# A two-layer attention backbone: transposes between the layers into the score banks, and a second `hf` buffer

## The chip, the cores and the metric

The kernel runs on one core of one Trainium2 chip. The metric is the device time of one execution, in microseconds (us); of several runs the median is told. Engines are named as in the profile: PE is TensorE (PEld its weight loads), DVE is VectorE, ACT is ScalarE, POOL is GpSimd, SP is SyncE, which issues most DMAs.

## The reference, cut to what matters

A residual stream of 512 latent tokens and 256 context tokens, each 1024 wide, passes two layers. Layer 0 is differential attention, layer 1 grouped-query attention. Each layer normalises the stream, scales and shifts it by values derived from a conditioning vector, mixes it, and adds a normalised, gated result back:

```python
for i in range(DEPTH):
    h = rms_norm(x, pre_g[i]) * (1.0 + scale) + shift
    hc = rms_norm(xc, pre_g[i]) * (1.0 + cscale) + cshift
    ...                                     # y, yc = attention(h, hc) @ w_out
    x = x + gate * rms_norm(y, post_g[i])
    if not last:
        xc = xc + cgate * rms_norm(yc, post_g[i])
```

Everything is float32. The change lies where layer 0's last two lines meet layer 1's first two.

## The kernel before, in words

Tokens are worked on in six tiles of 128 (0 to 3 latent, 4 and 5 context). A float32 product is made of three matmuls on operands split in a high and a low part (`mm3`, L142 to L145: high by high, high by low, low by high), so every weight and every activation is cast to its high part on ACT and has its low part made by a subtraction on DVE or POOL (L203 and L204 for weights).

**PSUM.** The eight banks are divided by hand (L120, L121): four single banks `bk`, and two score tiles `sc` of two banks each. The four single banks are handed out in turn from a list `lru`: `pj` (L129) takes the bank at its head for an accumulation and `close` (L135) puts it back at the end after its readers were issued; `trp` (L124) takes the head for transposes and puts it at the end at once. `sc2` (L138) hands out the two score tiles in turn. Score tiles serve the attention scores, the opening's transposes (L568) and the first four output projections of layer 0 (L1069).

**The stage of the change.** After layer 0's attention, `w_out` is applied in three column groups (256, 256 and 512 wide). The last group's loop (L1254 to L1263) goes over the six token tiles. For tile i it takes a bank, multiplies the first four of eight row blocks (12 matmuls), transposes the first half of tile i-2 (`h1_tr(.., 0)`), multiplies the other four blocks, calls `resid_a` (L1210: sum of squares on ACT, multiplication by the gate into `u` on DVE, then the bank is closed), transposes the second half of tile i-2, and calls `resid_b` (L1222: the new residual on DVE, its sum of squares on ACT, the reciprocal root and the normalised tokens `xn` on POOL).

`h1_tr(m, j)` (L1237) turns half j of the normalised tile m (four blocks of 128 columns) to feature-major form: four transposes on PE into one bank (L1241), then scale and shift per block into the SBUF buffer `hf`, two blocks on DVE (L1247, HFD = 2) and two on ACT (L1249), then the cast of all four to the high part on ACT (L1251) and the subtraction for the low part on DVE (L1252). `hf` exists once (`bufs=1`).

Tiles 4 and 5 are transposed later, inside the list `KV` (L44, loop from L1331), which orders layer 1's k projections ('k'), v projections ('v'), transposes of rotated keys ('c') and of tiles 4 and 5 ('t') by hand. Each k or v projection takes a bank with `pj` and needs `h1hi` and `h1lo` of its token tile, and the split weights 8 and 9 (k) or 10 and 11 (v), which come through weight slots that the last group of `w_out` leaves.

**What sets the order.** The program text gives each instruction a priority (its place in the text, moved ahead inside `hot` and `tc.high_priority`), and the framework's scheduler, which plans the whole program ahead by a timeline of its own, fixes each engine's order. On the chip every engine takes its instructions in that fixed order and waits on semaphores that the framework places.

Of the kernel before, what the change touches and what calls it, by code (L numbers as in the profile page):

```python
# [9 lines left out]
F32 = mybir.dt.float32  # L10
# [6 lines left out]
P = 128  # L17
# [59 lines left out]
def f32(ap):  # L77
    return ap.bitcast(F32)
# [3 lines left out]
def tile_backbone(  # L82
# [23 lines left out]
    def nm(s):  # L106
        uid[0] += 1
        return f"{s}_{uid[0]}"
# [15 lines left out]
    def trp():  # L124
        i = lru.pop(0)
        lru.append(i)
        return banks[i]
# [10 lines left out]
    def sc2():  # L138
        scs.append(scs.pop(0))
        return scs[-1]  # L140
# [1009 lines left out]
    bp = bp_stack.enter_context(tc.tile_pool(name="bp", bufs=1))  # L1150
# [71 lines left out]
    def resid_b(m):  # L1222
# [11 lines left out]
        nc.gpsimd.tensor_scalar(t, xd, r, 1.0, ALU.mult, ALU.mult)  # L1234
        xn[m] = t

    def h1_tr(m, j):  # L1237
        v = 0 if m < NQ else 1
        tr = trp()
        for k in range(4):  # L1240
            nc.tensor.transpose(tr[:, k * P:(k + 1) * P], xn[m][:, (j * 4 + k) * P:(j * 4 + k + 1) * P], ident)  # L1241
        hf = bp.tile([P, 4, P], F32, tag="hf", name=nm("hf"), bufs=1)
        for k in range(4):
            kt = j * 4 + k
            src, s_, h_ = tr[:, k * P:(k + 1) * P], mods[:, 1, v, 1, kt:kt + 1], mods[:, 1, v, 0, kt:kt + 1]
            if k < HFD:
                nc.vector.tensor_scalar(hf[:, k, :], src, s_, h_, ALU.mult, ALU.add)  # L1247
            else:
                nc.scalar.activation(hf[:, k, :], src, AF.Identity, scale=s_, bias=h_)  # L1249
        hs = h1hi[:, j * 4:j * 4 + 4, m * P:(m + 1) * P]  # L1250
        nc.scalar.copy(hs, hf)  # L1251
        nc.vector.tensor_tensor(h1lo[:, j * 4:j * 4 + 4, m * P:(m + 1) * P], hf, f32(hs), ALU.subtract)  # L1252

    for i, m in enumerate(order):  # L1254
        o = pj(n)
        run(out_proj(o, ghi, glo, w, m, n, 0, 4))
        if i >= 2:
            h1_tr(order[i - 2], 0)
        run(out_proj(o, ghi, glo, w, m, n, 4, 8))
        resid_a(m, o)  # L1260
        if i >= 2:
            h1_tr(order[i - 2], 1)
        resid_b(m)  # L1263
# [3 lines left out]
    with tc.tile_pool(name="t1", bufs=1, side="right") as t1p:  # L1267
# [63 lines left out]
        for what, m in KV:  # L1331
            if what == "t":
                hot(h1_tr, m, 0)
                hot(h1_tr, m, 1)
            elif what == "c":
                k_tr(*ktr.pop(0))
            elif what == "g":
                gate1_acc()
            else:
                if what == "v" and wv is None:  # L1340
                    wv = (ws.get(10), ws.get(11))
                o = pj(256)
                run(proj_tok(o, wk if what == "k" else wv, m))
                if late:
                    k_rope(*late.pop())
                if what == "k":
                    late.append((m, o, head_rstd(o)))
                else:
                    nc.scalar.copy(vh[:, m, :], o)
                    nc.vector.tensor_tensor(vl[:, m, :], o, f32(vh[:, m, :]), ALU.subtract)  # L1350
                    close(o)
# [172 lines left out]
        for h in range(KT):  # L1524
            p, j = h // 2, h % 2
# [142 lines left out]
```

## Time and profile before

| | |
|---|---|
| median of three runs | 836.27 us (836.08 to 836.4) |
| the profiled execution | 835.36 us |
| its span in the trace | 833.4 us |
| mean granted TensorE clock | 0.992 |
| PE, DVE, ACT, POOL busy | 96%, 58%, 55%, 53% of the span |

The profile lists busy time per engine, groups of equal instructions, waits (who waited for whom, and which instruction ended the wait) and instructions in order of time. An output is named before its inputs, `bk<-ident,xn` being a transpose of `xn` into a single bank; buffer numbers are left out. In windows, a row gives a stretch of time and each engine's busy time in it. A wait for several semaphores is put down to the one that came last. Ends of matmuls are modelled, so that those that run one behind the other overlap on paper.

### The profile page before, as it was taken

How to read it: one execution, taken by the hardware profiler on the slowest of the kernel's cores; microseconds unless marked ns; L12 is line 12 of the kernel's file. 1: busy time of each engine (PE TensorE's matmuls, PEld its weight loads, DVE VectorE, ACT ScalarE, POOL GpSimd, SP SyncE). 2: the span in 40 equal slices, each digit the busy share in tenths (PEclk: the TensorE clock that was granted, in tenths of full speed). 3: DMA queues.
4: the chain of work that ended last, by engine and by line, in shares of the span. 5: the costliest groups of instructions: out<-in, count | busy, mean ns of one | idle time of the engine just before them, and what ended most of it. 6: DMA issues, size and time to landing. Idle time of an engine off the chain costs nothing. (4 is left out here: it accounts for less than half of the span.)

```text
span 833.4 us, 14405 instructions
## 1 busy us (share of the span) xinstructions
PE 797.3 (96%) x5482; PEld 705.0 (85%) x5482; DVE 482.7 (58%) x897; ACT 457.5 (55%) x1001; POOL 438.2 (53%) x538
## 2 busy tenths in 40 slices
PE   7999999999999999999999999789999999999997
PEld 5688887798878898778988898678999889899986
DVE  4434576764857525674477857566346656665634
ACT  5424357674574644764467642575355665666731
POOL 4444755865475843765733202576677755543201
PEclk9899999999999999999999999999999999999999
DMA  9934211122233321414310066040221210210212
GB/s 300 351 116 140 76 39 42 63 99 66 75 102 125 116 76 64 143 48 154 126 51 26 27 242 212 1 133 25 78 77 52 77 51 1 77 51 26 66 36 101
DMA packets 41540, 77.77 MB, mean 93 GB/s; under 512 B 3584, under 2 KB 18688, under 8 KB 41472
## 3 DMA queue, kind: packets, MB, share of 16 engines
q1 hardware_dynamic: 38048, 71.71, 25.8%
q10 hardware_dynamic: 3424, 5.15, 1.8%
q8 instruction: 43, 0.70, 0.4%
q14 instruction: 25, 0.20, 0.1%
HBM read 70.56 MB, written 2.10 MB: 87 GB/s over the span
## 5 line engine op out<-in xcount | busy, mean ns | idle before, releaser
L197 POOL TENSOR_TENSOR wlo<-raw,whi 128x256 fp32r<-128x256 f32 x200 | 148.9, 776 | 89.5 <-ACT whi L203 81.0
L143 PE MATMUL bk<-whi,h 128*128 128x256 f32 (+1 forms) x592 | 177.3, 302 | 7.7 <-ACT hf L1249 4.9
L144 PE MATMUL bk<-wlo,h 128*128 128x256 f32 (+1 forms) x592 | 177.0, 300 | 0.2 <-DVE wlo L197 0.2
L145 PE MATMUL bk<-whi,h 128*128 128x256 f32 (+1 forms) x592 | 175.8, 300 | 1.0 <-DVE h L1252 1.0
L143 PE MATMUL bk<-h,whi 128*128 128x512 f32 (+2 forms) x416 | 147.5, 355 | 2.1 <-ACT sq L962 1.5
L144 PE MATMUL bk<-h,whi 128*128 128x512 f32 (+2 forms) x416 | 144.9, 349 | 0.0
L145 PE MATMUL bk<-h,wlo 128*128 128x512 f32 (+2 forms) x416 | 144.8, 348 | 0.1
L143 PEld LDWEIGHTS bk<-whi,h 128*128 128x128 f32 x592 | 113.0, 191 | 18.0 <-ACT hf L1249 5.8
L144 PEld LDWEIGHTS bk<-wlo,h 128*128 128x128 f32 x592 | 113.0, 191 | 4.4 <-issue 0.5
L145 PEld LDWEIGHTS bk<-whi,h 128*128 128x128 f32 x592 | 112.1, 190 | 5.3 <-DVE h L1252 1.6
L211 POOL TENSOR_SCALAR p<-p,sm 128x768 f32<-128x768 f32 (+1 forms) x80 | 68.0, 852 | 81.8 <-DVE sm L876 34.5
L143 PEld LDWEIGHTS bk<-h,whi 128*128 128x128 f32 x416 | 78.2, 188 | 14.6 <-issue 4.5
L203 ACT CAST whi<-raw 128x1024 fp32r<-128x1024 f32 x64 | 67.2, 1050 | 36.9 <-PE bk L144 14.9
L145 PEld LDWEIGHTS bk<-h,wlo 128*128 128x128 f32 x416 | 78.1, 188 | 8.7 <-issue 1.3
L144 PEld LDWEIGHTS bk<-h,whi 128*128 128x128 f32 x416 | 78.3, 188 | 7.0 <-issue 0.8
L873 ACT ACTIVATE p<-sc,sm 128x768 f32<-128x768 f32 (+1 forms) x68 | 59.6, 880 | 29.4 <-DVE sm L870 28.6
L870 DVE TENSOR_REDUCE sm<-sc 128x1 f32<-128x768 f32 (+1 forms) x68 | 60.5, 919 | 22.0 <-PE sc L865 22.0
L1457 DVE TENSOR_TENSOR al<-bk,ah 128x512 fp32r<-128x512 f32 x48 | 32.3, 687 | 33.4 <-ACT ah L1456 33.2
L933 ACT CAST ah<-bk 128x512 fp32r<-128x512 f32 x56 | 31.7, 591 | 29.7 <-PE bk L930 23.3
L934 DVE TENSOR_TENSOR al<-bk,ah 128x512 fp32r<-128x512 f32 x56 | 37.6, 684 | 16.4 <-ACT ah L933 15.9
L865 PE MATMUL sc<-qk,qk 64*128 64x384 f32 (+1 forms) x396 | 46.1, 355 | 0.2 <-POOL qk L765 0.2
L181 POOL TENSOR_TENSOR sz<-sz,za 128x384 f32<-128x384 f32 (+1 forms) x24 | 28.1, 1174 | 32.9 <-ACT za L180 32.9
(245 smaller groups left out, 1697.4 us busy)
## 6 DMA issues: line engine op xcount, KB each, us to landing
raw<-in_a_w SPq DMA_DIRECT2D x30, 512.0 KB, 3.5
araw<-in_ada_w SPq DMA_DIRECT2D x12, 1024.0 KB, 5.3
raw<-in_b_w SPq DMA_DIRECT2D x20, 512.0 KB, 3.5
ag<-in_ada_w SPq DMA_DIRECT2D x32, 256.0 KB, 6.9
raw<-in_w_out SPq DMA_DIRECT2D x16, 512.0 KB, 3.5
sw<-qr ACTq DMA_DIRECT2D x32, 128.0 KB, 2.1
gw<-in_ada_w SPq DMA_DIRECT2D x8, 512.0 KB, 4.3
xt<-in_x SPq DMA_DIRECT2D x4, 512.0 KB, 5.4
```

The costliest lines, as they stand in the source:

```text
L143: nc.tensor.matmul(o, ahi, bhi, start=start, stop=False)
L144: nc.tensor.matmul(o, ahi, blo, start=False, stop=False)
L145: nc.tensor.matmul(o, alo, bhi, start=False, stop=stop)
L197: eng.tensor_tensor(dst[:, i:i + n], a[:, i:i + n], b[:, i:i + n], op)
L203: nc.scalar.copy(hi, r)
L211: (nc.vector if eng == "v" else nc.gpsimd).tensor_scalar(dst, src, s_, 1.0, ALU.mult, ALU.mult)
L865: prev = nc.tensor.matmul(sc[m][:, j if nk == T else m, :w], a[r, tok], b[r, c], start=i == 0, stop=i == 2)
L870: nc.vector.tensor_reduce(mx, scv, AX.XY if nk == T else AX.X, ALU.max, negate=True)
L873: nc.scalar.activation(pv_, scv, AF.Exp, bias=mx, accum_out=l[:, m:m + 1])
L933: nc.scalar.copy(ah, tr)
L934: nc.vector.tensor_tensor(al, tr, f32(ah), ALU.subtract)
L1457: nc.vector.tensor_tensor(al, tr, f32(ah), ALU.subtract)
```

## The change

`h1_tr` no longer takes a bank from the four with `trp`. With the first half of a tile it takes a score tile with `sc2`; the first half's transposes go to the first bank of that tile and the second half's to the second. The SBUF buffer `hf` exists twice. Nothing else in the text differs.

```diff
+    h1_ps = {}
+
     def h1_tr(m, j):
         v = 0 if m < NQ else 1
-        tr = trp()
+        if j == 0:
+            h1_ps[m] = sc2()
+        tr = h1_ps[m][:, j, :]
         for k in range(4):
             nc.tensor.transpose(tr[:, k * P:(k + 1) * P], xn[m][:, (j * 4 + k) * P:(j * 4 + k + 1) * P], ident)
-        hf = bp.tile([P, 4, P], F32, tag="hf", name=nm("hf"), bufs=1)
+        hf = bp.tile([P, 4, P], F32, tag="hf", name=nm("hf"), bufs=2)
```

## The prediction, made before the result was known

> **What bounds the kernel now.** I read the page first, then the stage between the layers by windows, then what TensorE waits for there, then its order of time.
>
> ```profile
> span 833.4 us, 14405 instructions
> ...
> PE 797.3 (96%) x5482; PEld 705.0 (85%) x5482; DVE 482.7 (58%) x897; ACT 457.5 (55%) x1001; POOL 438.2 (53%) x538
> ```
>
> ```profile
> 490.00:525.00 35.00, 34.69 (x207) 30.40 (x206) 22.11 (x35) 10.63 (x36) 9.98 (x21) 1.00 0.69 240
> 525.00:580.00 55.00, 46.49 (x305) 40.55 (x304) 36.01 (x78) 34.47 (x93) 36.39 (x56) 0.97 0.16 52
> 580.00:600.00 20.00, 20.00 (x170) 20.00 (x169) 4.74 (x15) 7.07 (x21) 12.07 (x21) 1.00 0.32 103
> ```
>
> The page first: TensorE (PE) is busy 96% of an 833.4 us span, so the whole kernel is a queue of matmuls and only its gaps are for sale. The windows (columns: stretch, length, then busy time and instructions of PE, PEld, DVE, ACT, POOL, then granted clock) show where one lies. Before 525 us PE is busy 34.69 of 35 us and from 580 us all 20 of 20. Between them it is busy 46.49 of 55: 8.5 us of gaps, in the stretch that the change touches. No other engine is full there: DVE 36.01 of 55 (65%), ACT 34.47 (63%). The stage is a chain of waits, not of work. Whose waits:
>
> ```profile
> PE bk L143 <- ACT hf L1249: 4.9, 4, 3.8
> PE bk L143 <- DVE u L1214: 1.1, 1, 1.1
> PE bk L145 <- DVE h L1252: 1.0, 3, 0.4
> PE bk L1241 <- DVE u L1214: 0.7, 1, 0.7
> PE bk L143 <- ACT h L1251: 0.6, 1, 0.6
> PE bk L1311 <- DVE kn L1321: 0.2, 1, 0.2
> ```
>
> Columns are microseconds in total, times, longest. A matmul of L143 opens an accumulation in a fresh bank and reads no `hf`; so "L143 <- ACT hf" can only mean that its bank still held transposed tokens that ACT had not read. The same goes for "<- DVE u" (a bank that still held a projection). These three rows, 4.9 + 1.1 + 0.7 = 6.7 us, are waits for a bank. The other three, 1.0 + 0.6 + 0.2 = 1.8 us, are waits for data: `h` itself, or a rotated key. The longest wait alone is 3.8 us. Its story in order of time (start, duration):
>
> ```profile
> 525.31 1.04 PE L1241 MATMUL bk<-ident,xn 128*128 128x128 f32 x8
> 526.62 0.72 DVE L1247 TENSOR_SCALAR hf<-bk,mods 128x128 f32<-128x128 f32 x2
> 527.43 0.80 ACT L1249 ACTIVATE hf<-bk,mods 128x128 f32<-128x128 f32 x2 [1.46 <-DVE hf L1247]
> 527.70 1.25 PE L1241 MATMUL bk<-ident,xn 128*128 128x128 f32 x8
> 529.66 0.60 ACT L1251 CAST h<-hf 128x512 fp32r<-128x512 f32 x1
> 530.30 0.69 DVE L1252 TENSOR_TENSOR h<-hf,h 128x512 fp32r<-128x512 f32 x1 [0.68 <-ACT h L1251]
> 531.10 0.73 DVE L1247 TENSOR_SCALAR hf<-bk,mods 128x128 f32<-128x128 f32 x2
> 531.92 0.81 ACT L1249 ACTIVATE hf<-bk,mods 128x128 f32<-128x128 f32 x2 [0.46 <-DVE hf L1247]
> 532.78 0.50 PE L143 MATMUL bk<-whi,h 128*128 128x512 f32 x1 [3.83 <-ACT hf L1249]
> 533.12 0.40 PE L144 MATMUL bk<-wlo,h 128*128 128x512 f32 x1
> 533.35 0.40 PE L145 MATMUL bk<-whi,h 128*128 128x512 f32 x1
> ```
>
> At 525.31 both halves of token tile 0 are transposed (eight transposes), each half in a bank of its own. DVE and ACT turn the first half into `hf` (526.62, 527.43), ACT casts it (529.66), DVE subtracts (530.30 to 530.99). Only then may the second half begin, since there is one `hf` buffer: DVE at 531.10, ACT from 531.92 to 532.73. PE had nothing since about 529, and starts token tile 4 at 532.78, 0.05 us after that read. Follow the four banks in the order in which they are handed out, calling them a to d: tile 0 takes a, tile 1 b, tile 2 c, its two transposes (of tile 0) d and a, tile 3 b, its transposes d and c, tile 4 again a. So tile 4 waits for the second half of tile 0 to leave bank a, and that half waits for the one `hf` buffer. The change takes away both links.
>
> **The change part by part.** *The banks.* The transposes keep their number and length; only their destination moves, and with it one claimant fewer turns the four banks: tile 4 then gets the bank of tile 0, finished long before. Are the score banks free?
>
> ```profile
> 493.00:600.00 107.00, 0.00 (x0) 0.00 (x0) 0.00 (x0) 0.00 (x0) 0.98 0.34 113
> ```
>
> That is the busy time of instructions that touch a score bank: none on any engine from 493 to 600 us. So all 6.7 us of bank waits lose their cause, since the first k projections also open in banks that only projections used.
>
> *The clock.* After the 3.8 us gap the granted clock fell:
>
> ```profile
> 534.00:537.20 3.20, 3.20 (x9) 2.43 (x9) 2.43 (x5) 1.93 (x6) 1.52 (x4) 0.50 0.00 0
> 550.00:580.00 30.00, 27.11 (x214) 25.38 (x214) 20.30 (x50) 17.82 (x52) 21.78 (x31) 1.00 0.19 59
> ```
>
> Half speed for 3.2 us is 1.6 us of matmul time. The stage's other waits are at most 1.1 us long by the rows of waits, and from 550 to 580 us, among several of them, the clock read 1.00. So when the long gap goes, this goes: 6.7 + 1.6 = 8.3 us.
>
> *The second `hf` buffer.* It adds no instruction. What it shortens is the conversion, whose work is in these groups of the stage (busy, mean ns of one, idle before); the last row, of the tile `hf`, has the first and last start:
>
> ```profile
> L1249 ACT ACTIVATE hf<-bk,mods 128x128 f32<-128x128 f32 x24 | 9.6, 453 | 10.1 <-DVE hf L1247 9.9
> L1252 DVE TENSOR_TENSOR h<-hf,h 128x512 fp32r<-128x512 f32 x12 | 9.1, 758 | 7.9 <-ACT h L1251 7.9
> L1247 DVE TENSOR_SCALAR hf<-bk,mods 128x128 f32<-128x128 f32 x24 | 8.7, 405 | 1.2 <-PE bk L1241 0.5
> L1251 ACT CAST h<-hf 128x512 fp32r<-128x512 f32 x12 | 7.4, 618 | 0.2
> L1247 DVE TENSOR_SCALAR hf<-bk,mods x24: 401/403/411, 526.6 to 575.0; 128x128 f32<-128x128 f32 x24
> ```
>
> Twelve halves cost DVE 8.7 + 9.1 = 17.8 us and ACT 9.6 + 7.4 = 17.0 us, so 1.5 us of each per half; through one buffer they came 4.4 us apart (526.6 to 575.0 in eleven steps). With two buffers the next half's first pass may run while the cast is on ACT.
>
> *What is late next.* PE now reaches the k projections about 8 us sooner, and these need `h`. The data waits of 1.8 us stay in the sum; how much they grow no row shows. From below it is nothing: in a stage of 55 - 8 = 47 us DVE would be busy 36.01/47 = 77% and ACT 73%, still short of full. From above it is all 8.3 us: if the conversion kept its old pace, the last of tile 3 would come when it did,
>
> ```profile
> 562.87 0.39 PE L145 MATMUL bk<-whi,h 128*128 128x256 f32 x1 [0.44 <-DVE h L1252]
> ```
>
> and PE would stand at the same k projection until 562.87 again. I take 2 us, near the low end, because both links of the old pace are cut and the shares stay under four fifths.
>
> *Waits that the change adds.* Both halves of a tile now share one two-bank score tile, and tiles m and m+2 share it in turn. Is a two-bank tile waited for by banks, or as one? The kernel's opening transposes into the same tiles:
>
> ```profile
> 10.28 0.68 DVE L578 COPY xnt<-sc 128x512 f32<-128x512 f32 x1
> 10.99 0.59 ACT L576 COPY xnt<-sc 128x512 f32<-128x512 f32 x1 [0.46 <-DVE xnt L578]
> 13.44 1.06 PE L571 MATMUL sc<-ident,xt 128*128 128x128 f32 x8 [0.34 <-DVE xt L211]
> 14.62 0.69 DVE L578 COPY xnt<-sc 128x512 f32<-128x512 f32 x1 [0.72 <-PE sc L571]
> ```
>
> DVE copies the first bank, ACT the second. At 10.99 ACT starts 0.03 us after DVE's copy ended, having idled 0.46 us for it, although it reads the other bank. At 14.62 DVE, idle 0.72 us, starts only after the last of all eight transposes (13.44 + 1.06 = 14.50), not after the four that fill its bank. So waits run by pair. Then the second half's transposes stand in PE's queue until the first half has been read (tile 0: from 525.8, half of the eight, to ACT's 527.43 + 0.80, 2.4 us). Behind them in that queue stand the matmuls of a later projection tile, and for these wait ACT's sum of squares, DVE's `u` and the next `xn`. Between a tile's two halves the program issues 12 matmuls of the projection; by the starts at 533.12 and 533.35 that is 12 x 0.23 = 2.8 us, which covers 2.4 us where the order of the program is kept. I count what is left of this inside the 2 us. [...]
>
> *Queues.* No DMA is added or moved in the text of the program; SP's loads of b_w and of the last context tile hang on weight slots and on `xn`, which PE frees sooner, so they come sooner with it.
>
> Sum: 8.3 - 2 = 6.3 us off the profiled execution. Its own time is 835.36 us (span 833.4 and 1.96 around it), which gives 829.1. The median of the runs before is 836.27, 0.9 above the profiled one; set off from that, the forecast is 830.0 us.
>
> **The rivals.** *All of it (by banks):* the pair costs nothing and the conversion keeps up: 836.3 - 8.3 = 828.0. For it: the engine shares. Against: the opening rows. Chance 0.13.
>
> *The weights are late:*
>
> ```profile
> 545.11 2.11 POOL L1234 TENSOR_SCALAR gate<-gate,sm 128x1024 f32<-128x1024 f32 x1
> 547.19 3.31 POOL L197 TENSOR_TENSOR wlo<-raw,whi 128x256 fp32r<-128x256 f32 x4
> 549.49 0.39 PE L143 MATMUL bk<-whi,h 128*128 128x256 f32 x1 [1.07 <-DVE u L1214]
> 556.36 3.27 POOL L197 TENSOR_TENSOR wlo<-raw,whi 128x256 fp32r<-128x256 f32 x4
> ```
>
> POOL's split of the second k weight runs until 550.50, a microsecond past the start of the k projections at 549.49, and the second v weight until 559.63. Both follow the last projection tile through a freed slot, so they move with it, but POOL makes the normalised tile 4 just ahead, and that took 2.11 us. One such wait at k and one at v, 1 to 2 us each, leave 2.3 to 4.3 us of the 6.3: about 833. Chance 0.17.
>
> *Nothing comes of it:* the conversion keeps its old pace because DVE and ACT take their instructions in an order in which the second buffer is not used; then only waits after 562.87 are saved: 836 us. Chance 0.09.
>
> *Slower:* the pair wait decides. If the second half's transposes are queued right behind the first half's (as at 525.31, eight in a row), each of six tiles holds PE for the 2.4 us above: 14.4 us against 8.3 gained, +6 us, 842. It turns from gain to loss where the wait passes 8.3 / 6 = 1.4 us per tile. Against it: the 12 matmuls between the halves in program order. Since the order of every later instruction is planned anew, a shift of layer 1 adds to this case. Chance 0.11.
>
> **How the numbers follow.** The forecast (829 to 832 us) has 0.50, with 0.13, 0.17, 0.09 and 0.11 for the rivals in their order. 0.2% is 1.7 us, about what a measurement of this kernel can tell from no change. Faster: 0.50 + 0.13 + 0.17 = 0.80; same 0.09; slower 0.11. The range runs from just below "all of it", 827.2, to the "nothing" case, 836.4; outside are the slower case and a tail below.
>
> **What would show it.** Right: in the profile after, no "L143 <- ACT hf" or "<- DVE u" among PE's waits of this stage, no window at half clock near 535, the first 256-wide matmul of the k projections at about 541 instead of 549.49, and the stage's PE gaps at 2 to 4 us. The pair wait would show as "PE L1241 <- ACT hf" with score tiles as outputs; the late weights as "L144 <- POOL wlo"; an unchanged conversion as starts of L1247 still 4.4 us apart. Wrong would be the forecast if the gaps went and the end did not move by the same amount, that is, if layer 1 gave it back.

## The result, and the profile after

The changed kernel took 829.37 us (median of 6 runs, 827.1 to 830.14) against 836.17 us for the kernel before (6 runs, 834.73 to 836.97). The ratio is 0.9916, with a 95% interval from 0.9904 to 0.9928: 6.8 us faster, where 6.3 had been forecast. The profiled execution took 828.93 us.

From line 1241 on, the lines of the changed kernel stand four further down: the transposes are L1245, `hf` is written at L1251 (DVE) and L1253 (ACT), `h` at L1255 and L1256.

First the page of the changed kernel: span and busy time.

```profile
span 827.1 us, 14389 instructions
PE 796.6 (96%) x5482; PEld 706.2 (85%) x5482; DVE 484.0 (59%) x897; ACT 455.5 (55%) x1001; POOL 437.2 (53%) x538
```

The span is 6.3 us shorter. PE was idle for 833.4 - 797.3 = 36.1 us before and for 827.1 - 796.6 = 30.5 us after: 5.6 us of the gain are idle time, 0.7 us busy time. Next the windows, in the columns of those before (stretch, length, PE, PEld, DVE, ACT, POOL, granted clock):

```profile
525.00:580.00 55.00, 51.89 (x353) 47.30 (x352) 38.53 (x80) 36.07 (x100) 40.19 (x61) 0.97 0.18 60
```

The gaps of PE between 525 and 580 us fell from 8.5 to 55 - 51.89 = 3.1 us, so 5.4 of the 5.6 us come from the stage that was changed. Who is still waited for there (total, times, longest):

```profile
PE bk L145 <- DVE h L1256: 2.0, 1, 2.0
PE bk L144 <- DVE wlo L197: 0.6, 1, 0.6
PE sc L1245 <- POOL gate L1234: 0.4, 1, 0.4
```

All three waits for a bank are gone (4.9 + 1.1 + 0.7 us before). The waits for data are 2.0 + 0.6 + 0.4 = 3.0 us, where they were 1.8. PE's order of time in the changed kernel, with the transposes of tiles 0 to 2, the first k projection and the row that ends the 2.0 us wait:

```profile
526.85 0.60 PE L1245 MATMUL sc<-ident,xn 128*128 128x128 f32 x4
...
531.71 0.60 PE L1245 MATMUL sc<-ident,xn 128*128 128x128 f32 x4
...
533.07 0.60 PE L1245 MATMUL sc<-ident,xn 128*128 128x128 f32 x4
...
540.04 0.60 PE L1245 MATMUL sc<-ident,xn 128*128 128x128 f32 x4
...
540.95 0.60 PE L1245 MATMUL sc<-ident,xn 128*128 128x128 f32 x4
...
541.62 0.40 PE L143 MATMUL bk<-whi,h 128*128 128x256 f32 x2
...
546.80 0.60 PE L1245 MATMUL sc<-ident,xn 128*128 128x128 f32 x4
...
555.56 0.39 PE L145 MATMUL bk<-whi,h 128*128 128x256 f32 x1 [2.03 <-DVE h L1256]
```

The k projections start at 541.62 us; before it was 549.49. But the halves of a tile, which stood together before (eight transposes at 525.31), are now far apart: tile 0 at 526.85 and 533.07, tile 1 at 531.71 and 540.95, tile 2 at 540.04 and 546.80. That has a consequence on SP's queue. The load of tile 5's context in the changed kernel, and then the same in the kernel before:

```profile
547.43 0.33 SPq L1219 DMA_DIRECT2D xn<-in_xc  x1
```

```profile
541.46 0.34 SPq L1219 DMA_DIRECT2D xn<-in_xc  x1
```

The load is written into the `xn` buffer that tile 2 leaves. Tile 2's last transpose ended at 546.80 + 0.60 = 547.40, and the load was issued 0.03 us later, 6 us later than before. VectorE's order in the changed kernel shows what that meets:

```profile
549.18 1.36 DVE L1251 TENSOR_SCALAR hf<-sc,mods 128x128 f32<-128x128 f32 x4
551.94 2.44 DVE L1228 SCALAR_TENSOR_TENSOR xn<-u,sm,xn 128x512 f32<-128x512 f32 x2 [1.41 <-DMA xn<-in_xc]
554.30 1.81 DVE L1256 TENSOR_TENSOR h<-hf,h 128x512 fp32r<-128x512 f32 x2
```

At 551.94 VectorE had idled 1.41 us for that load, with two subtractions for `h` queued behind it. The residual of tile 5 (L1228) took 2.44 us, the first subtraction began at 554.30, and PE waited for it until 555.56. Before, at the same instruction of VectorE:

```profile
551.33 1.42 DVE L1228 SCALAR_TENSOR_TENSOR xn<-u,sm,xn 128x512 f32<-128x512 f32 x2 [1.89 <-POOL sm L387]
```

There the two took 1.42 us, and no wait of PE for `h` in the stage was over 0.6 us.

### The profile page after: what moved, and what is told of

Its sections match the earlier page's. It is cut to its first block, busy times and chain, and to the rows that moved or that the text cites. A ratio compares the mean times of both kernels' runs of the same rounds, so it can differ in the third digit from the quotient of the medians.

```text
span 827.1 us, 14389 instructions
## 1 busy us (share of the span) xinstructions
PE 796.6 (96%) x5482; PEld 706.2 (85%) x5482; DVE 484.0 (59%) x897; ACT 455.5 (55%) x1001; POOL 437.2 (53%) x538
## 5 line engine op out<-in xcount | busy, mean ns | idle before, releaser
L197 POOL TENSOR_TENSOR wlo<-raw,whi 128x256 fp32r<-128x256 f32 x200 | 149.3, 779 | 81.1 <-ACT whi L203 71.8
L143 PEld LDWEIGHTS bk<-whi,h 128*128 128x128 f32 x592 | 112.7, 190 | 10.2 <-issue 4.2
```

Of the source, the lines that this page charges most:

```text
L143: nc.tensor.matmul(o, ahi, bhi, start=start, stop=False)
L197: eng.tensor_tensor(dst[:, i:i + n], a[:, i:i + n], b[:, i:i + n], op)
```

## The experiments

**Theories.** A, that of the prediction: the gain is the waits for single banks, and the second `hf` buffer only helps. B: the gain is the second buffer. Beside them stood the question of whether a score tile is waited for as a pair, and what that costs. Twelve runs were made: the table has ten of them, beside the two kernels compared, and two more (split_ktr with another `HFD`) stand further down. Each was made beside the kernel before on the same chip, which gave 835.9 to 836.4 us; ratios are to that, with 95% intervals.

| run | token transposes | key transposes | `hf` | us (median) | ratio |
|---|---|---|---|---|---|
| before | single banks | single banks | 1 | 836.2 | 1 |
| banks_only | pair in a score tile | single banks | 1 | 840.50 | 1.0026 to 1.0069 |
| buffer_only | single banks | single banks | 2 | 832.17 | 0.9938 to 0.9970 |
| after | pair in a score tile | single banks | 2 | 829.37 | 0.9904 to 0.9928 |
| split_tiles | two score tiles | single banks | 2 | 832.34 | 0.9938 to 0.9975 |
| forced_pair | pair, halves adjacent | single banks | 2 | 843.94 | 1.0072 to 1.0116 |
| forced_split | two score tiles, adjacent | single banks | 2 | 831.61 | 0.9929 to 0.9966 |
| x5_behind | as after | single banks | 2 | 830.71 | 0.9917 to 0.9963 |
| buffer_ktr | single banks | score tiles | 2 | 830.52 | 0.9914 to 0.9959 |
| ktr_score | pair in a score tile | score tiles | 2 | 828.05 | 0.9885 to 0.9915 |
| split_ktr | two score tiles | score tiles | 2 | 826.31 | 0.9864 to 0.9897 |
| after_again | as after | single banks | 2 | 827.72 | 0.9877 to 0.9922 |

### Each part alone: banks_only and buffer_only

banks_only takes the second buffer back, buffer_only the banks:

```diff
-        hf = bp.tile([P, 4, P], F32, tag="hf", name=nm("hf"), bufs=2)
+        hf = bp.tile([P, 4, P], F32, tag="hf", name=nm("hf"), bufs=1)
```

```diff
-        if j == 0:
-            h1_ps[m] = sc2()
-        tr = h1_ps[m][:, j, :]
+        tr = trp()
```

> The changed kernel with its transposes in the score tiles, but one hf buffer as before. Theory A (the gain is the bank waits of TensorE and the clock that fell after the longest): 829 to 831 us, the first k projection at 541 to 543 us, no L143 <- ACT hf among the waits; data waits on h grow by 1 to 2 us. Theory B (the gain is the second hf buffer): 835 to 837 us, since nothing that B counts is changed.

> The kernel before with the second hf buffer, its transposes still in the four single banks. Theory A in its strict form (a bank must be free, whoever frees it): the second half of tile 0 is read some 3 us earlier through the second buffer, so the 3.8 us wait shrinks to about 1 us, too short for the clock to fall; the waits for u stay: 831 to 833 us. Theory B (the buffer is all of the gain): 829 to 830 us. If the buffer is of no use alone: 836 us.

Neither theory held. The banks alone made the kernel 4.5 us slower (840.50 against 836.03 beside it), the buffer alone 3.9 us faster, and both together 6.8 us faster: the parts do not add up. Waits of PE in banks_only (500 to 600 us):

```profile
PE sc L1245 <- ACT hf L1253: 3.4, 1, 3.4
PE sc L1245 <- POOL xn L1234: 2.5, 1, 2.5
PE bk L144 <- DVE wlo L197: 2.2, 1, 2.2
```

The waits for single banks are gone here too, but L1245 waits 3.4 us for ACT to read the first half of a tile (at 561.74), and 2.5 us for `xn`. That is the wait for the pair, and the one buffer lets the first half be read only late. Most of the 4.5 us is clock, though. The stage's window:

```profile
525.00:580.00 55.00, 45.34 (x277) 40.21 (x276) 35.29 (x72) 30.72 (x85) 31.83 (x51) 0.91 0.15 51
```

PE's gaps are 55 - 45.34 = 9.7 us, only 1.2 more than the 8.5 before. But the granted clock is 0.91 where it was 0.97: 10.2 us at half clock in place of 3.4, which is up to 3.4 us more. The conversion itself got slower; VectorE's first pass over the halves in banks_only, in the changed kernel and in buffer_only (first and last start):

```profile
L1251 DVE TENSOR_SCALAR hf<-sc,mods x24: 396/402/411, 527.1 to 584.0; 128x128 f32<-128x128 f32 x24
```

```profile
L1251 DVE TENSOR_SCALAR hf<-sc,mods x24: 395/400/409, 528.0 to 568.6; 128x128 f32<-128x128 f32 x24
```

```profile
L1249 DVE TENSOR_SCALAR hf<-bk,mods x24: 394/402/411, 525.8 to 571.8; 128x128 f32<-128x128 f32 x24
```

Over eleven steps that is (584.0 - 527.1)/11 = 5.2 us from half to half in banks_only, 3.7 us after, 4.2 us in buffer_only, 4.4 us before. In buffer_only the 3.8 us wait has gone, and other waits for single banks have come:

```profile
PE bk L1243 <- POOL qrs L1302: 2.6, 1, 2.6
PE bk L1243 <- DVE kn L1323: 1.3, 1, 1.3
PE bk L143 <- ACT h L1253: 1.0, 1, 1.0
```

Two k projections hold their banks until POOL's `qrs` and VectorE's `kn` are done, and the transposes of tile 4 wait 2.6 and 1.3 us for them. So the buffer cures the wait of tile 4's projection, and the banks cure what then comes next; the banks need the buffer first.

### The wait for the pair: forced_pair and forced_split

In both, the halves of tiles 0 to 3 are transposed together, and the next projection's matmuls are ordered behind the second half. For that `h1_tr` returns its last transpose, which becomes `e1`. forced_pair keeps the score tile of the changed kernel; forced_split puts half j into score tile j. The loop of both, then what forced_split has besides:

```diff
     for i, m in enumerate(order):
         o = pj(n)
-        run(out_proj(o, ghi, glo, w, m, n, 0, 4))
+        with after(e1):
+            run(out_proj(o, ghi, glo, w, m, n, 0, 4))
         if i >= 2:
             h1_tr(order[i - 2], 0)
-        run(out_proj(o, ghi, glo, w, m, n, 4, 8))
+            e1 = h1_tr(order[i - 2], 1)
+        with after(e1):
+            run(out_proj(o, ghi, glo, w, m, n, 4, 8))
         resid_a(m, o)
-        if i >= 2:
-            h1_tr(order[i - 2], 1)
         resid_b(m)
```

```diff
-        if j == 0:
-            h1_ps[m] = sc2()
-        tr = h1_ps[m][:, j, :]
+        tr = scs[j][:, m % 2, :]
```

> The changed kernel with both halves of tiles 0 to 3 transposed together and TensorE's next projection matmuls ordered behind the second half. If a score tile is waited for as one (the slower rival of the prediction): TensorE stands 2.0 to 2.5 us at each second half, shown as L1245 <- ACT hf, four times, 8 to 10 us, and the clock falls after some: 836 to 842 us. If single banks are waited for: no such wait, 829 to 831 us.

> The kernel of forced_pair (halves of tiles 0 to 3 adjacent, the next projection matmuls behind them), but the halves in two different score tiles. If the 6.3 us of L1245 <- ACT hf in forced_pair (2.9, 1.7, 1.7) were the wait for the pair: that row is gone, and with two losses of clock the time falls by 6 to 10 us against forced_pair's 843.9, to 834 to 838 us; the 4.4 us wait for xn at 523.5 us, which the forced order causes, stays. If they came from the forced order: the waits stay, 842 to 844 us.

Waits of PE in forced_pair, then in forced_split:

```profile
PE sc L1245 <- ACT hf L1253: 6.3, 3, 2.9
PE sc L1245 <- POOL xn L1234: 5.4, 2, 4.4
```

```profile
PE sc L1243 <- POOL xn L1234: 4.4, 1, 4.4
```

With the pair, PE waits three times for ACT's reading of the first half, 2.9, 1.7 and 1.7 us (tile 3 kept 34 matmuls between its halves in the planned order). With two tiles that row is gone, and the time is 12.3 us lower, 2 us better than expected; half of that is the row itself, the rest half clock (10.2 us in this stage with the pair, 6.8 without) and waits further on. So a score tile is waited for as one, and a second half that has nothing ahead of it pays 1.7 to 2.9 us; the prediction had put it at 2.4.

### Halves in different tiles: split_tiles and split_ktr

split_tiles is the changed kernel with the second diff above alone. split_ktr also moves the transposes of rotated keys; ktr_score does only that:

```diff
-            tr = trp()
+            tr = sc2()[:, 0, :]
             for j in range(2):
                 nc.tensor.transpose(tr[:, j * P:(j + 1) * P], kr[:, j * P:(j + 1) * P], ident)
```

> The changed kernel, but the two halves of a token tile go to two different score tiles (half j to tile j, bank m % 2), so that a second half need not wait for the reading of the first. If the wait by pair costs time in the changed kernel (it sends second halves late: 6.2 us after the first for tile 0, 9.2 for tile 1; these delay tile 3's h and, through xn, the load of tile 5's context): the 2.0 us wait for h near 555 us and the half clock behind it (3.8 us, so 1.7 us lost) go, 826 to 828 us. If it costs nothing: 829.4 us as the changed kernel, within 0.8.

> split_tiles with the transposes of rotated keys in the score tiles too. split_tiles lost 1.8 us waiting for a single bank that a key's transposes held (L143 <- DVE kl), 0.9 us for one that a k projection held (kn), and half clock behind the first (1.7 us). If those banks are why it lost against the changed kernel (832.3 against 829.4 us): 828 to 830 us. If it is the late tile 5 and a worse order of layer 1: 831 to 833 us.

> The changed kernel with the transposes of rotated keys in the score tiles too (first bank of each). In the changed kernel no wait for a single bank is left in the stage, so this should bring nothing, 829.4 us within 1, and cost 1 to 2 us if pair waits between keys and tokens come in. If single banks still set the planned order: 827 to 828 us.

split_tiles did what was meant between 525 and 550 us, and was slower than the changed kernel all the same. Its waits and its first pass over the halves:

```profile
PE bk L143 <- DVE kl L1317: 1.8, 1, 1.8
PE sc L1243 <- POOL xn L1234: 1.0, 1, 1.0
PE bk L143 <- DVE kn L1323: 0.9, 1, 0.9
```

```profile
L1249 DVE TENSOR_SCALAR hf<-sc,mods x24: 393/402/411, 527.5 to 561.7; 128x128 f32<-128x128 f32 x24
```

The halves come (561.7 - 527.5)/11 = 3.1 us apart, and the long wait for `h` is gone. In its place PE waits 1.8 us for a single bank that a key's transposes hold until `kl` is made, and 0.9 us for one that a k projection holds. Moving the keys as well (split_ktr) takes the first row away and leaves the other two as they are. Its stage:

```profile
525.00:580.00 55.00, 51.78 (x374) 47.71 (x373) 38.73 (x82) 34.55 (x99) 41.74 (x62) 1.00 0.20 67
```

Its gaps of PE, 55 - 51.78 = 3.2 us, are no smaller than the 3.1 of the changed kernel. What it does not have is half clock in the stage. At 826.31 us it is the fastest kernel of this study, slightly better than expected. Moving the keys without splitting the pair (ktr_score, 828.05 us) looked like 1.3 us against the changed kernel's 829.37, but after_again ran the changed kernel at 827.72 us: no gain is shown. For split_ktr the interval lies apart from that of after and overlaps that of after_again, so its advantage, 1.4 to 3 us by the medians, is likely and not settled.

buffer_ktr moves the keys and leaves the tokens in the single banks (the second buffer kept):

> buffer_only (token transposes in the single banks, two hf buffers) with the transposes of rotated keys in the score tiles instead. If any claimant fewer at the single banks would do: 828 to 830 us. If it must be the token transposes, since the waits that buffer_only has left (2.6 and 1.3 us before the transposes of tile 4, for banks that k projections hold until POOL's qrs and VectorE's kn) come before the first key is transposed: those waits stay, 831 to 833 us.

Both waits of buffer_only are there again, 2.6 and 1.3 us, as the second reading said. The time, 830.52 us, lies between the two readings and cannot be told from 832.17.

Two more kernels change `HFD` in split_ktr from 2 to 1 and to 3, which moves a quarter of the first pass between VectorE and ScalarE.

> split_ktr with one block of each half scaled on VectorE and three on ScalarE (two and two before): 12 x 0.4 = 4.8 us less for VectorE, 12 x 0.45 = 5.4 us more for ScalarE. If VectorE's load is what is left between the layers (38.7 of 55 us, ScalarE 34.6): 1 to 2 us faster than split_ktr, 824 to 825.5 us. If the chain through both engines is, ScalarE's third block lengthens it: 827 to 830 us.

> split_ktr with three blocks of each half on VectorE and one on ScalarE: 4.8 us more for VectorE, 5.4 us less for ScalarE. If VectorE's load is what is left: slower, 828 to 831 us. If neither engine's load is and only the order of instructions counts: 826 us within 1, as with one block.

They took 826.70 us (0.9864 to 0.9903) and 827.52 us (0.9880 to 0.9917): neither can be told from 826.31. The load of these two engines is not what is left; the longest wait in both is for POOL's `xn` of tile 5:

```profile
PE sc L1243 <- POOL xn L1234: 1.3, 1, 1.3
```

```profile
PE sc L1243 <- POOL xn L1234: 1.9, 1, 1.9
```

### What held `h` in the changed kernel: x5_behind

VectorE's residual of tile 5 is queued behind the `h` of tile 3's first half (`h1_tr` returns its last instruction for that):

```diff
-            h1_tr(order[i - 2], 0)
+            e1 = h1_tr(order[i - 2], 0)
...
-        resid_b(m)
+        with after(e1 if i == 5 else None):
+            resid_b(m)
```

> The changed kernel with one order changed on VectorE: the residual of tile 5 (L1228, 2.4 us, which waited 1.4 us for its load) is queued behind the subtractions for h of tile 2's second and tile 3's first half instead of ahead of them. If it was what held h: the 2.0 us wait for h at 555.56 us and the half clock of 3.8 us behind it (1.7 us) go, less about 1 us for a later tile 5: 826 to 828 us. If h is late for another reason (the conversion's own pace): the wait stays, 829 to 831 us.

VectorE's order, then PE's waits in this kernel:

```profile
551.83 2.04 DVE L1256 TENSOR_TENSOR h<-hf,h 128x512 fp32r<-128x512 f32 x2 [1.81 <-ACT h L1255]
553.79 1.88 DVE L1228 SCALAR_TENSOR_TENSOR xn<-u,sm,xn 128x512 f32<-128x512 f32 x2
555.60 1.35 DVE L1251 TENSOR_SCALAR hf<-sc,mods 128x128 f32<-128x128 f32 x4
```

```profile
PE sc L1245 <- ACT hf L1253: 2.8, 1, 2.8
```

The cause was right: `h` comes at 551.83 instead of 554.30, and PE no longer waits for it. The worth of it was not: the residual now stands ahead of the first pass over tile 3's second and tile 4's first half (555.60), and the transposes of tile 4's second half wait 2.8 us for the first half to be read. The wait for the pair took the place of the wait for `h`: from 525 to 580 us the half clock is gone (1.00), but the gaps of PE grew from 3.1 to 55 - 49.18 = 5.8 us, and 830.71 us is no faster than the changed kernel.

### The clock: after_again

Half clock was counted in windows of 0.2 us over the whole span of the traces. It comes in stretches of 3.4 us, or of twice that, at 0.50, so one of 3.4 us costs at most 1.7 us of matmul time. The end of the span left out, the changed kernel has four, the kernel before one of double length near its start beside the one at 534 us. Windows that lie inside three of the four of the changed kernel (the other starts at 31.2 us), then inside the one of the kernel before:

```profile
10.80:14.00 3.20, 3.20 (x19) 2.06 (x18) 2.32 (x4) 1.59 (x3) 1.59 (x3) 0.50 1.14 330
434.20:437.20 3.00, 3.00 (x17) 2.78 (x18) 2.05 (x3) 0.17 (x1) 0.52 (x1) 0.50 0.00 0
557.00:560.20 3.20, 3.20 (x17) 3.20 (x16) 1.58 (x6) 3.17 (x13) 2.53 (x5) 0.50 0.43 164
```

```profile
18.60:25.20 6.60, 6.60 (x23) 5.79 (x24) 3.21 (x6) 2.03 (x3) 2.99 (x4) 0.50 1.09 361
```

> The changed kernel, unchanged, profiled once more. The first profile lost 1.7 us of TensorE time in each of four stretches of half clock (from 10.6, 31.2, 434.0 and 556.8 us). If a stretch follows from the waits of the program alone: the same four again, above all the one behind the 2.0 us wait for h, and a profiled time within 0.5 us of 828.9. If it also depends on when in a window of some 3.4 us a wait falls, which no program sets: other stretches, and a profiled time that differs by steps of about 1.7 us.

The same kernel, profiled a second time:

```profile
32.40:35.60 3.20, 3.20 (x16) 3.20 (x16) 1.59 (x3) 3.03 (x7) 1.75 (x3) 0.50 1.10 348
434.20:437.20 3.00, 3.00 (x26) 2.61 (x26) 2.77 (x5) 0.43 (x1) 0.23 (x1) 1.00 0.00 0
554.80:557.80 3.00, 3.00 (x16) 3.00 (x16) 1.38 (x5) 2.32 (x9) 2.55 (x4) 0.50 0.65 197
```

```profile
554.20 0.39 PE L145 MATMUL bk<-whi,h 128*128 128x256 f32 x1 [2.15 <-DVE h L1256]
```

The wait for `h` came again (2.15 us), with half clock behind it. Of the other three stretches only one did; at 434 us the clock was 1.00. Two stretches fewer would be up to 3.4 us, but the profiled execution took 827.40 us, only 1.5 less than the first. That is the stretch at 434 us alone. At the same transposes of L930 ahead of it the two executions stood 0.3 us apart (427.36 and 427.07 us), and behind it 1.8 us (437.86 and 436.07). The other stretch that the first execution had more lay near the start and is part of those 0.3 us: there PE was not what held the kernel up. So the second reading held for the stretches outside the stage, and the first for the one inside. A single profiled time can carry such a step.

## Why the prediction was right, point by point

**The waits for banks** (6.7 us): all gone, as said, and the k projections came at 541.62 us for a forecast of about 541.

**The clock** (1.6 us): this term failed. The step was "when the long gap goes, this goes", on the ground that the other waits were 1.1 us at most. The stretch at 534 us went, but behind the new wait of 2.0 us stood another, at 557 us. The term was worth nothing.

**What is late next** (2 us): the mechanism was right, `h` being waited for, and the size was off. The waits for data grew by 1.2 us (1.8 to 3.0); the half clock behind them stands against the clock term above. Inside 525 to 580 us the sum is 8.5 - 3.1 = 5.4 us of gaps and no clock, where 6.3 was forecast. How long the whole stage took is read from two matmuls that are the same in both kernels, one of `w_out` ahead of the stage and the first score matmul of layer 1. Before, then after:

```profile
492.84 0.39 PE L143 MATMUL bk<-whi,h 128*128 128x256 f32 x1 [0.32 <-ACT jk L1184]
...
616.00 0.34 PE L143 MATMUL sc<-kh,qh 128*128 128x384 f32 x1
```

```profile
494.38 0.39 PE L143 MATMUL bk<-whi,h 128*128 128x256 f32 x1 [0.32 <-ACT jk L1184]
...
610.61 0.34 PE L143 MATMUL sc<-kh,qh 128*128 128x384 f32 x1
```

From the one to the other it is 123.2 us before and 116.2 after: 6.9 us gained, 1.5 more than the gaps show. No term of the forecast has these 1.5 us. An estimate of where they lie: a 512-wide matmul is drawn 0.40 us long, but in a stream the next starts 0.23 us behind it (533.12 and 533.35 us in the kernel before), so each wait hides some 0.17 us in busy time, and 8 waits fewer (11 before, 3 after) are 1.4 us. Against the gain stands that the changed kernel came to the stage 1.5 us later (494.38 for 492.84), by the half clock at 434 us that its second execution did not have. With 0.9 us from layer 1 (below) the sum is 6.9 - 1.5 + 0.9 = 6.3 us, the fall of the span. Part of the match with 830.0 is therefore luck: the clock term was lost, 2.4 us that nobody had forecast came in for it, and 1.5 us were lost to a half clock that this one execution happened to have.

**The second buffer**: the prediction let the banks carry the gain ("so all 6.7 us of bank waits lose their cause"). It is true of these waits, and false of the time: the banks alone cost 4.5 us. The condition that it passed over is that a pair of banks turns over only as fast as `hf` does.

**The wait for the pair**: right that it exists and by its size. The reason why it would be covered, 12 matmuls between the halves "where the order of the program is kept", failed: the planner does not keep that order. For tiles 0 to 2 it moved the second halves 6.2 to 9.2 us behind the first, far enough to cover the wait, and so far that other things came late. "Slower" was one diff away: in banks_only for lack of the buffer (+4.5 us), in forced_pair for lack of cover (+7.9 us against the kernel run beside it).

**Queues**: "so they come sooner with it" failed for one load of two. The weights came sooner (POOL's split of the second k weight at 542.80 us for 547.19 before), and the late weights cost one wait of 0.6 us. The context of tile 5 came 6 us later, since its buffer is freed by the second half of tile 2, which is what the planner had put off. That load stood behind the largest wait that was left in the stage.

**Layer 1** gave nothing back: from its first score matmul to the end of the span it took 833.4 - 616.0 = 217.4 us before and 827.1 - 610.6 = 216.5 us after.

## What to carry to other kernels

A freed resource is worth what the next wait in line leaves of it: here the banks alone lost, the buffer alone gained some 4 of 7 us, and only both together gave the whole, so edits that touch one chain are weighed together. Before placing two pieces of work in one tile, ask what it is waited for as, a tile or its banks, and whether the planner will then move the second piece: the moved piece frees its own input late, and a load may hang on that. Read TensorE's gaps with the clock beside them, since a wait of 2 us may cost nearly twice its length (here 2.0 us, and up to 1.7 us in the half clock behind it).

## What the runs showed of the hardware

**Half clock behind a short wait.** In ktr_score PE waited 1.4 us for `h`, and was busy 1.95 of the 3.4 us ahead of the half clock; in x5_behind it waited 2.8 us (up to 558.25 us), and the clock stayed at 1.00. Windows of ktr_score, then of x5_behind:

```profile
551.30:554.70 3.40, 1.95 (x13) 1.53 (x13) 3.40 (x5) 2.31 (x9) 3.31 (x4) 1.00 0.12 34
554.80:558.00 3.20, 3.20 (x17) 3.06 (x16) 1.28 (x5) 2.54 (x10) 2.75 (x6) 0.50 0.44 168
```

```profile
553.46:556.87 3.41, 1.98 (x17) 1.77 (x15) 3.41 (x7) 1.82 (x6) 1.45 (x4) 1.00 0.33 129
556.88:560.29 3.41, 2.04 (x16) 1.92 (x17) 1.52 (x5) 3.30 (x15) 2.78 (x4) 1.00 0.20 65
```

The length of a wait alone does not decide, then. Where it falls seems to: within one trace the stretches of half clock begin whole multiples of 3.413 us apart (in the changed kernel at 10.76, 31.24, 434.01 and 556.89 us, which is 6, 118 and 36 lengths between them; the windows of 0.2 us in which they begin read 0.89, 0.59, 0.52 and 0.72, which gives the hundredths). In the kernel before it is 151 such lengths from 18.56 to 533.97 us, in after_again 153 from 32.35 to 554.58. The windows of x5_behind above are laid on the grid of its own stretch at 434.00 us. Its long wait lies across two of them, so that neither is emptier than 1.98 us, while the window of the changed kernel ahead of its half clock was busy 1.38 us (553.47 to 556.88). That is no threshold: in the kernel before, the window from 131.20 to 134.61 us was busy 1.79 us, and the clock stayed at 1.00, while ktr_score lost it behind 1.95 us. The program alone does not set the places either: outside the stage the changed kernel lost the clock from 10.76, 31.24 and 434.01 us in one execution, and in the second from 32.35 us alone. What else decides was not shown.

**VectorE beside POOL.** The two instructions of tile 5's residual took 2.44 us in the changed kernel, while POOL split a weight (L197, 551.27 to 554.96 us), and 1.42 us in the kernel before, where POOL stood idle meanwhile (from 551.3 to 552.9 us). In x5_behind POOL's split ended at 554.46 us, within the first of the two: the first took 1.22 us, the second 0.74. But in forced_pair the first took 0.79 us beside such a split. Whether the split has to do with the longer times is therefore not shown; no run was made to separate them.
